# Two-layer streaming trunk on one core: low parts and products moved to VectorE, and the last two w_down groups exchanged in size

## The chip, the cores and the metric

The kernel runs on one core of a Trainium2 chip, in one launch. The metric is the device time of a whole execution in microseconds (us), from the first to the last instruction of the program and what lies around it. The core has four computing engines with instruction streams of their own: TensorE (PE in the profile, with PEld for its weight loads), VectorE (DVE), ScalarE (ACT) and GpSimd (POOL); SyncE (SP) and GpSimd issue the DMA transfers.

## What is computed

Two layers over 576 tokens (64 of a later chunk, 512 of a first chunk), width 1024, feed-forward width 2816:

```
for l in range(2):
    xn = rmsnorm(x, norm_mix[l])
    x = x + merge_branches(three attentions of xn @ w_in[l]) 
    xn = rmsnorm(x, norm_ffn[l])
    gu = xn @ w_up[l]                        # (576, 2 * 2816)
    g, u = gu[:, :2816], gu[:, 2816:]
    c = conv_b + causal 3-tap convolution of g along the tokens
    x = x + (gelu(c) * u) @ w_down[l]
y = rmsnorm(x, norm_final)
```

The change lies in the feed-forward part of each layer, from `xn @ w_up` to the sum with `w_down`.

## The kernel before

Data lie transposed: 128 features on the partitions, 576 tokens along the row; `x` is eight such tiles, the feed-forward width 22 (f = 0 to 21). A float32 product is made from two rounded parts each: a high part (hi, a rounded copy) and a low part (lo, what the rounding left), and three matmuls of 128x128 by 128x288: hi by hi, hi by lo, lo by hi. `scalar.copy` makes a high part, a subtraction on VectorE the low one.

The first NORD = 4 tiles of each layer are made in the old form (`ffn_f`): 48 matmuls for the gate half (mg), 48 for the up half (mu), then the convolution (c, two VectorE passes of 128x578), gelu (ge on ScalarE), the product with `ur`, and the parts `hh` and `hl`. Meanwhile `forms` prepares block sums of x for the other 18 tiles (fh and fl). These are made as block products (`unit_f`): seven products of half size, A11, P, R, A12, Q, A22, V in this order, with 12 matmuls each, 84 for a tile. Their weights are sums of quarter blocks of w_up: `wforms` loads them (wr), adds them on VectorE and spawns `wparts`, which makes the parts: piece a holds A11 and A12 (whi..a, wlo..a), b holds P and R (eh..b, el..b), c holds Q and V (whi..c, wlo..c), d holds A22 (eh..d, el..d). The high and low tiles of a have two buffers that a and c share, so whi of tile f waits for A12 of tile f - 1. A low part is made in one of two ways:

```
def low(out, src, hi, by_dma):
    if by_dma:
        scalar.activation(out, hi.bitcast(F32), AF.Copy, scale=-1.0)
        charge("POOL", 900)
        nc.gpsimd.dma_start(out, src, accum_op=ALU.add)
    else:
        vector.tensor_tensor(out, src, hi.bitcast(F32), op=ALU.subtract)
```

The last product of a tile, V, gives the second half of the gate (gp); then follow c on ScalarE (one pass) and VectorE (two), gelu, ge * u, hh and hl.

The down product `x += hh, hl by w_down` (md, weights dr and dh, dl, or wrd and whid, wlod) runs in groups of f tiles, in four pieces d2 of two x tiles each: 12 matmuls for an x tile and group tile, so a piece has 24 matmuls in a group of two and 48 in a group of four. Between block-product tiles stands one piece of an earlier group. The last group ends the layer: in layer 0 each finished x tile gets its parts for the next layer's products (xhm on ScalarE, xlm on VectorE, squares added on GpSimd into accm), and the next products are mv1a; in layer 1 `down_final` goes through the last group by halves of the tokens and each finished half tile goes into facc and xg, then come transposes (y), the sum over the partitions (frp), the scale rr and the outputs.

The order of instructions on each engine is fixed when the program is built: steps are written as generators, and a planner with a clock per engine and costs per operation (`charge`) decides which generator goes next. On the chip every engine takes its instructions strictly in that order.

Of the kernel before, what the change touches and what calls it, by code (L numbers as in the profile page):

```python
# [14 lines left out]
ALU = mybir.AluOpType  # L15
# [23 lines left out]
EARLY = 2  # L39
XACT = ()  # L40
XADD = 3
FG = [2, 2, 4, 4, 4, 4, 2]
NORD = 4
GW = TOK + 4

# [2 lines left out]
def trunk_kernel(ctx: ExitStack, tc: tile.TileContext, a: dict, o: dict):  # L48
# [91 lines left out]
    vector = Engine(nc.vector, "DVE", dve_cost)  # L140
    gpsimd = Engine(nc.gpsimd, "POOL", pool_cost)
# [10 lines left out]
    def spawn(label, g, first=False):  # L152
        gens.insert(0 if first else len(gens), [label, g, cx["t"]])
# [1038 lines left out]
    def layer(l):  # L1192
# [65 lines left out]
        def ffn_f(f):  # L1258
            nm = f"{l}f{f}"
            t = {}  # L1260

            def pre():
                drain(f"f{l}{f - 2}")
                gp = slot(f"gp{nm}", w=GW)
                t["gp"] = gp
                gpsimd.tensor_copy(gp[:, 0:2], state(l, f))
                gpsimd.memset(gp[:, 66:68], 0.0)

            def evg(j, ps, cs, h):
                gp, R = t["gp"], cur["R"]  # L1270
                if h == 0:
                    vector.tensor_tensor(gp[:, 2:66], ps[:, 0:T], R[:, 0:T], op=ALU.mult)
                    vector.tensor_tensor(gp[:, 68:292], ps[:, T:HALF], R[:, T:HALF], op=ALU.mult)
                else:
                    vector.tensor_tensor(gp[:, 292:580], ps, R[:, cs], op=ALU.mult)

            def conv():
                t["ge"] = yield from conv_steps(f, t["gp"])

            def pre_u():  # L1280
                t["ur"] = ap_.tile([P, TOK], F32, tag="g", name=f"ur{nm}", bufs=2)

            def evu(j, ps, cs, h):
                vector.tensor_tensor(t["ur"][:, cs], ps, cur["R"][:, cs], op=ALU.mult)

            def fin():
                ge = t["ge"][:, 0:TOK]
                gpsimd.tensor_tensor(ge, ge, t["ur"], op=ALU.mult)
                yield
                h_, l_ = slot(f"hh{nm}", F32R), slot(f"hl{nm}", F32R)  # L1290
                scalar.copy(h_, ge)
                yield
                vector.tensor_tensor(l_, ge, h_.bitcast(F32), op=ALU.subtract)
                hs[f] = (h_, l_)

            chunk(f"g{nm}", a["w_up"][l][:, f * P:(f + 1) * P], ND, act, evg, pre_ev=pre,
                  pre=begin_ffn if f == 0 else (lambda: spawn("wf", wforms())) if f == NORD - 1 else None, norm=[1] if f == 0 else None,
                  post=lambda: (spawn(f"c{l}{f}", conv()), spawn("forms", forms()) if f == 0 else None))

            def post_u():  # L1300
                drain(f"c{l}{f}")
                spawn(f"f{l}{f}", fin())

            chunk(f"u{nm}", a["w_up"][l][:, F + f * P:F + (f + 1) * P], ND, act, evu, pre_ev=pre_u, post=post_u,
                  pre=(lambda: fast.update(last=True)) if f == NORD - 1 else None)
# [65 lines left out]
        def wparts(f, nm, forms_, src, by_dma, small):  # L1371

            if f > NORD:
                yield from until(lambda: all((f - 1, n) in used for n in forms_))
            elif nm == "a":
                yield from until(lambda: "last" in fast)
            elif nm in "cd":
                yield from until(lambda: "go" in fast)
            yield
            key = f"{l}{f}{nm}"  # L1380
            if small:
                pairs = [(half_tile(f"eh{key}{j}", F32R), half_tile(f"el{key}{j}", F32R))
                         for j in range(len(forms_))]
            else:
                h_, l_ = (wp.tile([P, 8, P], F32R, tag=t, name=f"{t}{key}", bufs=2) for t in ("whi", "wlo"))
                pairs = [(h_[:, 4 * j:4 * j + 4, :], l_[:, 4 * j:4 * j + 4, :]) for j in range(2)]
            for j, n in enumerate(forms_):
                hi, lo = pairs[j]
                scalar.copy(hi, src[:, 4 * j:4 * j + 4, :])
                yield  # L1390
                low(lo, src[:, 4 * j:4 * j + 4, :], hi, by_dma)
                ws[f, n] = (hi, lo)
                made.add((f, n))
                yield

        def wforms():

            w = a["w_up"][l]
            rr = lambda t: t.rearrange("(k p) c -> p k c", p=P)
            for f in range(NORD, NF):  # L1400
                gc, uc = w[:, f * P:(f + 1) * P], w[:, F + f * P:F + (f + 1) * P]

                def raw(i, *need):
                    if f > NORD:
                        yield from until(lambda: all((f - 1, n) in made for n in need))
                    return wp.tile([P, 8, P], F32, tag="raw", name=f"wr{l}{f}{i}", bufs=3)

                r1 = yield from raw(1, "P", "R")
                dma(r1[:, 4:8, :], rr(uc[0:D // 2]))
                r0 = yield from raw(0, "A11", "A12")  # L1410
                dma(r0, rr(gc))
                if f > NORD:
                    yield from until(lambda: (f - 1, "A22") in made)
                a22 = half_tile(f"wr{l}{f}3")
                dma(a22, rr(uc[D // 2:D]))
                yield from pause(6000)
                vector.tensor_tensor(r1[:, 0:4, :], r1[:, 4:8, :], a22, op=ALU.add)
                yield
                vector.tensor_tensor(r1[:, 4:8, :], r1[:, 4:8, :], r0[:, 0:4, :], op=ALU.add)
                yield  # L1420
                spawn("wa", wparts(f, "a", ("A11", "A12"), r0, f != NORD + 1, False), True)
                spawn("wb", wparts(f, "b", ("P", "R"), r1, False, True), True)
                spawn("wd", wparts(f, "d", ("A22",), a22, True, True), True)
                q = yield from raw(2, "Q", "V")
                vector.tensor_tensor(q[:, 0:4, :], r1[:, 0:4, :], r0[:, 0:4, :], op=ALU.add)
                yield
                vector.tensor_tensor(q[:, 4:8, :], q[:, 0:4, :], r0[:, 4:8, :], op=ALU.add)
                yield
                spawn("wc", wparts(f, "c", ("Q", "V"), q, False, False), True)
# [132 lines left out]
        def down(fs, last):  # L1562
            def ev(d2):
                def go(j, ps, cs, h):
                    d = 2 * d2 + j
                    if fs[0] == 0:
                        drain_while(lambda: fast.get("y", -1) < d % 4, "y")
                        cx["t"] = clk["PE"] + 70
                    vector.tensor_tensor(x[d][:, cs], ps, x[d][:, cs], op=ALU.add)
                    if last and h == 1:  # L1570
                        norm_tile(f"m{l + 1}", d, x[d], gmix(l + 1, d))
                        dma(xsp[d], x[d])
                return go

            if last or fs[0] == 0:
                for d2 in range(4):
                    chunk(f"d{l}{fs[0]}{d2}", down_w(fs, d2), len(fs),
                          lambda: ([hs[f][0] for f in fs], [hs[f][1] for f in fs]), ev(d2), ncol=2,
                          pre=down_pre(fs, d2, last))
                return  # L1580
            for d2 in range(4):
                yield
                own = fs is not groups[-2] or d2 < 2
                chunk(f"d{l}{fs[0]}{d2}", down_w(fs, d2), len(fs),
                      lambda: ([hs[f][0] for f in fs], [hs[f][1] for f in fs]), ev(d2), ncol=2,
                      pre=down_pre(fs, d2, last), post=lambda n=len(owns): issued.add(n), own=own)
                if own:
                    owns.append((chunks[-1], fs, d2))
# [18 lines left out]
        groups = []  # L1607
# [7 lines left out]
            for n, (c, fs, d2) in enumerate(owns):  # L1615
                yield from down_own(c, fs, d2, lambda: n == 0 or n - 1 in issued)

        downs = iter(())
        for gi, fs in enumerate(groups):
            for i, f in enumerate(fs):  # L1620
                if f < NORD:
                    ffn_f(f)
                    if gi and i == 0:
                        list(downs)
                    continue
                chunk(f"x{l}{f}", None, 0, lambda f=f: (f == NORD and start_fast(), unit_f(f)), None, own=True)
                next(downs, None)
            list(downs)
            downs = down(fs, False)
            if gi:  # L1630
                next(downs)

        def start_fast():
            drain("forms")
# [368 lines left out]
```

## Time and profile before

| | |
|---|---|
| median of 3 runs | 2208.74 us (2205.34 to 2210.13) |
| profiled execution | 2207.59 us |
| its span, first to last instruction | 2205.7 us |
| TensorE busy | 2111.8 us (96%) |
| VectorE, ScalarE, GpSimd busy | 1514.3, 1228.5, 425.3 us |
| granted TensorE clock, mean | 0.984 of full |

The rows below come from the profiled execution; 1.9 us of its time lie outside its span. A busy share near the whole says which engine sets the time, and what is to be had lies where that engine waits.

### The profile page before, as it was taken

How to read it: one execution, taken by the hardware profiler on the slowest of the kernel's cores; microseconds unless marked ns; L12 is line 12 of the kernel's file. 1: busy time of each engine (PE TensorE's matmuls, PEld its weight loads, DVE VectorE, ACT ScalarE, POOL GpSimd, SP SyncE). 2: the span in 40 equal slices, each digit the busy share in tenths (PEclk: the TensorE clock that was granted, in tenths of full speed). 3: DMA queues.
4: the chain of work that ended last, by engine and by line, in shares of the span. 5: the costliest groups of instructions: out<-in, count | busy, mean ns of one | idle time of the engine just before them, and what ended most of it. 6: DMA issues, size and time to landing. Idle time of an engine off the chain costs nothing.

```text
span 2205.7 us, 40108 instructions
## 1 busy us (share of the span) xinstructions
PE 2111.8 (96%) x15479; PEld 2069.2 (94%) x15479; DVE 1514.3 (69%) x3148; ACT 1228.5 (56%) x2485; POOL 425.3 (19%) x615
## 2 busy tenths in 40 slices
PE   8999999999999879999899999999999998799997
PEld 7999999999999779999899999999999997699997
DVE  7886657676558657777568766677765686567775
ACT  5657766555436435555346677755554464455554
POOL 2111221111213212222101122202102231221121
PEclk9999999999999989999999999999999999899999
DMA  7442222232424436556243322233323264456551
GB/s 216 124 144 70 79 81 78 83 104 83 129 78 114 114 92 148 134 137 142 80 117 95 97 71 71 71 102 90 96 77 120 86 131 102 101 142 146 129 125 59
DMA packets 346280, 234.87 MB, mean 106 GB/s; under 512 B 13872, under 2 KB 324082, under 8 KB 346026
## 3 DMA queue, kind: packets, MB, share of 16 engines
q1 hardware_dynamic: 325898, 194.88, 30.1%
q0 software_dynamic: 20192, 37.43, 9.5%
q8 instruction: 122, 2.00, 0.4%
q14 instruction: 68, 0.56, 0.1%
HBM read 176.54 MB, written 25.83 MB: 92 GB/s over the span
## 4 chain that ended last, share of the span: by engine, by line
PE 83%; DVE 5%; issue 5%; DMA 4%; ACT 2%; POOL 1%; SPq 0%; POOLq 0%; DVEq 0%; ACTq 0%
PE md L146 10%; PE mo L146 4%; PE mg1a L146 2%; PE mg0a L146 2%; PE mg1b L146 2%; PE mg0b L146 2%; PE mg1c L146 2%; PE mg0c L146 2%; PE mv1a L146 1%; PE mb0a L146 1%; PE mb1a L146 1%; PE mv1b L146 1%; PE mv0b L146 1%; PE mv0c L146 1%; PE mv1c L146 1%
## 5 line engine op out<-in xcount | busy, mean ns | idle before, releaser
L117 DVE TENSOR_TENSOR wr<-wr,wr 128x512 f32<-128x512 f32 x144 | 98.7, 688 | 69.2 <-DMA wr<-in_w_up 68.0
L117 DVE TENSOR_TENSOR x<-md,x 128x288 f32<-128x288 f32 x224 | 98.4, 453 | 37.2 <-PE md L146 36.8
L146 PE MATMUL mo<-ml,whio 128*128 128x288 f32 x256 | 75.8, 296 | 0.8 <-DVE ml L117 0.8
L146 PE MATMUL md<-hh0f,dl 128*128 128x288 f32 x256 | 75.6, 295 | 0.5 <-DVE dl L117 0.5
L146 PE MATMUL md<-hh1f,dl 128*128 128x288 f32 x256 | 75.6, 295 | 0.5 <-DVE dl L117 0.5
L146 PE MATMUL mo<-mh,whio 128*128 128x288 f32 x256 | 75.8, 296 | 0.0
L146 PE MATMUL md<-hh0f,dh 128*128 128x288 f32 x256 | 75.5, 295 | 0.0
L146 PE MATMUL md<-hl1f,dh 128*128 128x288 f32 x256 | 75.5, 295 | 0.0
L146 PE MATMUL md<-hh1f,dh 128*128 128x288 f32 x256 | 75.5, 295 | 0.0
L146 PE MATMUL md<-hl0f,dh 128*128 128x288 f32 x256 | 75.5, 295 | 0.0
L146 PE MATMUL mo<-mh,wloo 128*128 128x288 f32 x256 | 75.4, 295 | 0.0
L117 DVE TENSOR_TENSOR dl<-dr,dh 128x512 fp32r<-128x512 f32 (+1 forms) x72 | 45.2, 628 | 19.8 <-ACT dh L117 19.8
L146 PEld LDWEIGHTS mo<-ml,whio 128*128 128x128 f32 x256 | 48.2, 188 | 1.2 <-DVE ml L117 1.2
L146 PEld LDWEIGHTS md<-hh1f,dl 128*128 128x128 f32 x256 | 48.2, 188 | 0.8 <-DVE dl L117 0.8
L146 PEld LDWEIGHTS md<-hh0f,dl 128*128 128x128 f32 x256 | 48.2, 188 | 0.8 <-DVE dl L117 0.8
L146 PEld LDWEIGHTS md<-hh1f,dh 128*128 128x128 f32 x256 | 48.2, 188 | 0.0
L146 PEld LDWEIGHTS mo<-mh,wloo 128*128 128x128 f32 x256 | 48.2, 188 | 0.0
L146 PEld LDWEIGHTS md<-hl0f,dh 128*128 128x128 f32 x256 | 48.2, 188 | 0.0
L146 PEld LDWEIGHTS md<-hh0f,dh 128*128 128x128 f32 x256 | 48.1, 188 | 0.0
L146 PEld LDWEIGHTS md<-hl1f,dh 128*128 128x128 f32 x256 | 48.1, 188 | 0.0
L146 PEld LDWEIGHTS mo<-mh,whio 128*128 128x128 f32 x256 | 48.1, 188 | 0.0
L117 ACT ACTIVATE xhf<-x,pcol 128x576 fp32r<-128x576 f32 x16 | 12.5, 780 | 63.9 <-DVE x L117 63.9
(2902 smaller groups left out, 9493.1 us busy)
## 6 DMA issues: line engine op xcount, KB each, us to landing
wr<-in_w_up SPq DMA_DIRECT2D x72, 256.0 KB
wr<-in_w_up SPq DMA_DIRECT2D x36, 512.0 KB
dr<-in_w_down SPq DMA_DIRECT2D x56, 256.0 KB
wro<-in_w_out SPq DMA_DIRECT2D x16, 512.0 KB
xspill<-x SPq DMA_DIRECT2D x16, 288.0 KB
x<-xspill SPq DMA_DIRECT2D x16, 288.0 KB
wrg0a<-in_w_in SPq DMA_DIRECT2D x8, 512.0 KB
wrg0b<-in_w_in SPq DMA_DIRECT2D x8, 512.0 KB
```

Source lines behind the costliest of these rows:

```text
L117: return f(*args, **kw)
L146: nc.tensor.matmul(out, lhsT=lhsT, rhs=rhs, start=start, stop=stop, skip_group_check=True)
```

## The change

Three edits. The product `ge * ur` of the four old-form tiles of each layer goes from GpSimd to VectorE. The low parts of piece a go to VectorE for f = 4 to 9; before, VectorE made them for f = 5 alone and an accumulating DMA from GpSimd's queue for the others. The last two groups of w_down become two and four tiles, where they were four and two; the loop that puts pieces between tiles keeps a list of groups with open pieces, so that after tile 16 and 17 there stand pieces 0 and 1 of group 12 to 15, after 18 and 19 pieces 2 and 3 of it, after 20 and 21 pieces 0 and 1 of group 16 and 17, then its pieces 2 and 3, then the group of 18 to 21.

```diff
-FG = [2, 2, 4, 4, 4, 4, 2]
+FG = [2, 2, 4, 4, 4, 2, 4]
...
-                gpsimd.tensor_tensor(ge, ge, t["ur"], op=ALU.mult)
+                vector.tensor_tensor(ge, ge, t["ur"], op=ALU.mult)
...
-                spawn("wa", wparts(f, "a", ("A11", "A12"), r0, f != NORD + 1, False), True)
+                spawn("wa", wparts(f, "a", ("A11", "A12"), r0, f > NORD + 5, False), True)
...
-        downs = iter(())
+        waiting = []
         for gi, fs in enumerate(groups):
             for i, f in enumerate(fs):
                 if f < NORD:
                     ffn_f(f)
-                    if gi and i == 0:
-                        list(downs)
+                    if gi == 1 and i == 0:
+                        list(down(groups[0], False))
                     continue
                 chunk(f"x{l}{f}", None, 0, lambda f=f: (f == NORD and start_fast(), unit_f(f)), None, own=True)
-                next(downs, None)
-            list(downs)
-            downs = down(fs, False)
-            if gi:
-                next(downs)
+                if waiting and next(waiting[0], "end") == "end":
+                    waiting.pop(0)
+            if 0 < gi < len(groups) - 1:
+                waiting.append(down(fs, False))
+                next(waiting[-1])
+        for g in waiting:
+            list(g)
```

On VectorE, between V of tile 5 and the middle of tile 6 in layer 0, there stood before (gp is the second gate half of tile 5, x<-md the four evictions of the down piece, wr the sums for tile 6):

```order
L117 TENSOR_TENSOR gp0f_9073<-m0f5V,z0f_8882 128x288
L117 TENSOR_TENSOR wr_9218<-wr_9110,wr_9112 128x512
L117 TENSOR_TENSOR x_02_7486<-md_9214,x_02_7486 128x288
L117 SCALAR_TENSOR_TENSOR c0f_9220<-gp0f_9073,pcol_1178,c0f_9220 128x578 x2
L117 TENSOR_TENSOR x_02_7486<-md_9230,x_02_7486 128x288
L117 TENSOR_TENSOR el06b_9238<-wr_9110,eh06b_9237 128x512
L117 TENSOR_TENSOR wr_9218<-wr_9218,wr_9112 128x512
L117 TENSOR_TENSOR x_03_7488<-md_9253,x_03_7488 128x288
L117 TENSOR_TENSOR x_03_7488<-md_9263,x_03_7488 128x288
```

and in the change:

```order
L117 TENSOR_TENSOR gp0f_9071<-m0f5V,z0f_8876 128x288
L117 TENSOR_TENSOR wr_9216<-wr_9108,wr_9110 128x512
L117 TENSOR_TENSOR x_02_7486<-md_9212,x_02_7486 128x288
L117 SCALAR_TENSOR_TENSOR c0f_9218<-gp0f_9071,pcol_1178,c0f_9218 128x578 x2
L117 TENSOR_TENSOR x_02_7486<-md_9228,x_02_7486 128x288
L117 TENSOR_TENSOR el06b_9236<-wr_9108,eh06b_9235 128x512
L117 TENSOR_TENSOR wr_9216<-wr_9216,wr_9110 128x512
L117 TENSOR_TENSOR x_03_7488<-md_9251,x_03_7488 128x288
L117 TENSOR_TENSOR wlo06a<-wr_9110,whi06a 128x512
L117 TENSOR_TENSOR x_03_7488<-md_9260,x_03_7488 128x288
```

The low part wlo06a has come in behind the third eviction; nothing else has moved there. One tile later, on VectorE from the convolution of tile 6 to the first parts of tile 7, there stood before:

```order
L117 SCALAR_TENSOR_TENSOR c0f_9419<-gp0f_9271,pcol_1178,c0f_9419 128x578 x2
L117 TENSOR_TENSOR x_04_7490<-md_9429,x_04_7490 128x288
L117 TENSOR_TENSOR el07b_9437<-wr_9307,eh07b_9436 128x512
L117 TENSOR_TENSOR wr_9417<-wr_9417,wr_9320 128x512
L117 TENSOR_TENSOR x_05_7492<-md_9452,x_05_7492 128x288
L117 TENSOR_TENSOR x_05_7492<-md_9462,x_05_7492 128x288
L117 TENSOR_TENSOR dl_9484<-dr_9355,dh_9482 128x256
L117 TENSOR_TENSOR ge0f_9487<-ge0f_9487,u0f_9275 128x576
L117 TENSOR_TENSOR el07b_9439<-wr_9307,eh07b_9438 128x512
```

and in the change:

```order
L117 SCALAR_TENSOR_TENSOR c0f_9412<-gp0f_9268,pcol_1178,c0f_9412 128x578 x2
L117 TENSOR_TENSOR wr_9302<-wr_9302,wr_9332 128x512
L117 TENSOR_TENSOR x_04_7490<-md_9422,x_04_7490 128x288
L117 TENSOR_TENSOR x_05_7492<-md_9431,x_05_7492 128x288
L117 TENSOR_TENSOR x_05_7492<-md_9439,x_05_7492 128x288
L117 TENSOR_TENSOR wr_9460<-wr_9302,wr_9332 128x512
L117 TENSOR_TENSOR ge0f_9447<-ge0f_9447,u0f_9272 128x576
L117 TENSOR_TENSOR dl_9457<-dr_9363,dh_9455 128x256
L117 TENSOR_TENSOR el07b_9466<-wr_9302,eh07b_9465 128x512
L117 TENSOR_TENSOR wr_9460<-wr_9460,wr_9332 128x512
L117 TENSOR_TENSOR wlo07a<-wr_9332,whi07a 128x512
```

Two sums wr that stood ahead of gp have moved behind the convolution, ge stands ahead of the first el07b, and wlo07a comes last; tile 8 is ordered as tile 6. On ScalarE at tile 10 (c and ge are those of tile 9), the change has:

```order
L117 ACTIVATE c0f_10030<-gp0f_9891,pcol_1028,pcol_1178 128x578
L117 CAST eh010d_10042<-wr_9937 128x512
L117 CAST eh010b_10045<-wr_9913 128x512
L117 CAST whi010a<-wr_9935 128x512
L117 ACTIVATE el010d_10043<-eh010d_10042 128x512
L117 ACTIVATE wlo010a<-whi010a 128x512
```

This is the order that tile 9 had before; before the change whi010a and the first step of wlo010a stood ahead of c at tile 10.

## Rows read from the trace of the kernel before

**Rows 1.** Page, busy time and its share; costliest groups, busy us and mean ns.

```profile
PE 2111.8 (96%) x15479; PEld 2069.2 (94%) x15479; DVE 1514.3 (69%) x3148; ACT 1228.5 (56%) x2485; POOL 425.3 (19%) x615
...
L117 DVE TENSOR_TENSOR wr<-wr,wr 128x512 f32<-128x512 f32 x144 | 98.7, 688 | 69.2 <-DMA wr<-in_w_up 68.0
```

**Rows 2.** Waits of TensorE, whole span: us in total, times, longest.

```profile
PE md L146 <- DVE wlod L117: 9.3, 2, 5.8
...
PE md L146 <- DVE x L117: 4.0, 3, 1.8
...
PE m0f9A L146 <- DMA wlo09a<-wr: 2.6, 1, 2.6
...
PE m0f5A L146 <- DVE wlo05a L117: 2.2, 1, 2.2
...
PE m0f4A L146 <- DMA wlo04a<-wr: 1.4, 2, 0.7
```

**Rows 3.** Stretches: length, busy us (count) by engine, granted clock, DMA share, GB/s.

```profile
726.20:857.55 131.35, 105.09 (x698) 101.58 (x697) 79.73 (x143) 58.35 (x124) 26.02 (x46) 0.91 0.47 109
743.60:762.10 18.50, 16.33 (x108) 15.89 (x108) 14.52 (x28) 8.11 (x19) 1.86 (x5) 0.91 0.32 86
762.10:786.75 24.65, 17.80 (x109) 17.08 (x108) 12.59 (x24) 9.21 (x21) 3.65 (x7) 0.86 0.38 86
837.20:857.55 20.35, 17.80 (x134) 17.56 (x133) 13.87 (x27) 11.14 (x23) 6.61 (x10) 1.00 0.74 157
857.55:875.00 17.45, 17.45 (x134) 17.45 (x133) 13.00 (x25) 10.13 (x20) 3.54 (x7) 1.00 0.59 142
1815.95:1948.40 132.45, 106.00 (x699) 102.44 (x698) 80.40 (x143) 58.22 (x124) 25.98 (x46) 0.91 0.47 109
1061.15:1120.20 59.05, 46.66 (x295) 45.41 (x294) 34.40 (x64) 22.13 (x39) 9.17 (x7) 0.86 0.29 91
2152.20:2205.70 53.50, 40.92 (x301) 38.27 (x300) 29.72 (x62) 24.96 (x57) 10.37 (x13) 0.95 0.19 60
```

**Rows 4.** Timeline at tiles 6, 7, 9 of layer 0: start, us, instruction, idle before.

```profile
767.98 0.61 PE L146 MATMUL m0f6A<-fh,wlo06a 128*128 128x288 f32 x1 [5.32 <-DMA wlo06a<-wr]
792.62 0.61 PE L146 MATMUL m0f7A<-fh,wlo07a 128*128 128x288 f32 x1 [5.33 <-DMA wlo07a<-wr]
840.20 0.40 PE L146 MATMUL m0f9A<-fh,wlo09a 128*128 128x288 f32 x1 [2.55 <-DMA wlo09a<-wr]
763.71 0.82 DVE L117 TENSOR_TENSOR x<-md,x 128x288 f32<-128x288 f32 x2
790.07 0.69 DVE L117 TENSOR_TENSOR el07b<-wr,eh07b 128x512 fp32r<-128x512 f32 x1
836.86 0.45 DVE L117 TENSOR_TENSOR x<-md,x 128x288 f32<-128x288 f32 x1
```

**Rows 5.** Timeline of VectorE and GpSimd at an old-form product.

```profile
673.60 0.45 DVE L117 SCALAR_TENSOR_TENSOR tp<-tp,yb 128x288 f32<-128x288 f32 x1
674.08 1.57 DVE L117 TENSOR_TENSOR tq<-tp,yb 128x288 f32<-128x288 f32 x1
673.83 1.50 POOL L117 TENSOR_TENSOR ge0f<-ge0f,ur0f 128x576 f32<-128x576 f32 x1 [4.12 <-DVE ur0f L117]
```

**Rows 6.** Timeline of VectorE at the end of layer 0.

```profile
1088.41 0.82 DVE L117 SCALAR_TENSOR_TENSOR xlm<-x,pcol,xhm 128x576 fp32r<-128x576 f32 x1 [0.85 <-ACT xhm L117]
...
1090.81 0.82 DVE L117 SCALAR_TENSOR_TENSOR xlm<-x,pcol,xhm 128x576 fp32r<-128x576 f32 x1 [0.84 <-ACT xhm L117]
1091.54 1.62 DVE L117 TENSOR_TENSOR wlod<-wrd,whid 128x256 fp32r<-128x256 f32 x1
```

**Rows 7.** Timeline, the last eviction of x, and the chain that ended last behind it.

```profile
2191.39 0.46 DVE L117 TENSOR_TENSOR x<-md,x 128x288 f32<-128x288 f32 x1 [0.35 <-PE md L146]
...
2194.77 2.98 PE y L150 x25
2197.76 0.51 PE frp L146 x6
```

## The prediction

> **What bounds the kernel now.** I read the page's busy times first: TensorE is busy for 2111.8 us of 2205.7, VectorE for 1514.3 [rows 1]. So there are some 94 us in which TensorE stands still, and beside them only what it loses at a lower clock. The list of TensorE's waits says for what it stands: low parts of piece a that come by accumulating DMA (wlo04a, wlo09a and others of their kind), wlo05a from VectorE, and md waiting for wlod and for x [rows 2]. The third view, busy time by stretch, shows where. Tile 10 of layer 0 has no gap: 84 matmuls of the tile and 48 of a down piece in 17.45 us, 0.132 us for one, at granted clock 1.00 [rows 3]. A tile with a piece of 24 is then 108 × 0.1322 = 14.28 us of work, and tiles 4 to 9 (four with 24, two with 48) are 4 × 14.28 + 2 × 17.45 = 92.0. They took 131.35 us in layer 0 and 132.45 in layer 1, at granted clock 0.91: losses of 39.3 and 40.4 [rows 3]. The end of layer 0, from V of tile 21 to the middle of mv1a, took 59.05 us for 295 matmuls (39.0 of work), the end of layer 1 53.5 us [rows 3]. These four stretches hold most of what is lost, and the change touches each.
>
> **What a tile's loss is made of.** Tile 6 took 24.65 us, 10.4 over its work: a wait of 5.32 for wlo06a, and 4.4 to 5 that no wait covers, at granted clock 0.86 (1.2 GHz for part of the tile, 2.4 for the rest) [rows 3, 4]. Tile 9 waited 2.55 and lost 20.35 − 17.45 = 2.9 in all, at granted clock 1.00; tile 5 waited 2.2 for a low part that VectorE makes already, and lost 18.5 − 14.28 = 4.2 [rows 2 to 4]. A wait of some 2 us thus brings 0.35 to 2.0 more, mean 1.2; one of 5 brings over 4.
>
> **Low parts of piece a.** Tile 5 had its low part on VectorE before, so five tiles of a layer change. Each loses two scaled copies on ScalarE and two accumulating DMAs from GpSimd's queue, and gains two subtractions on VectorE. I price one as the sum wr of the same shape, two inputs in SBUF, 688 ns [rows 1]: 20 more, 14 us in 2200 on an engine 69% busy. What counts is where they stand in its order.
> - Tile 6: PE would take the low at 767.98 − 5.32 = 762.66. The low now stands behind the third eviction; the double row of the last two starts at 763.71, so the third ends near 764.15, the low near 764.8 [rows 4]. Wait 2.1, with 1.2 behind it 3.3 (before 10.4).
> - Tile 7: PE is ready at 792.62 − 5.33 = 787.29. Before, the last el07b ended at 790.07 + 0.69 = 790.76 [rows 4]. Now two wr have come behind the convolution (+1.38), a first-parts el fewer stands ahead (−0.69) and the low comes last (+0.69): 790.8 if the queue's own idle time takes the wr up, 792.1 if not: a wait of 3.5 to 4.8. I take 4.7, since gp and the convolution ahead leave the queue no slack, and 2.0 behind it: 6.7.
> - Tile 8 has tile 6's order: 3.3.
> - Tile 9: ready at 840.20 − 2.55 = 837.65; the eviction ends at 836.86 + 0.45 = 837.31, two wr and the low follow, 839.2 [rows 4]. Wait 1.5 and 0.4: 1.9.
> - Tile 4: two waits of 0.7 before [rows 2]; I leave 1.0 (bounds 0 to 3). Tile 5: nothing of its own changes, 4.2.
> - Tile 10 is still by DMA, but ScalarE now starts its first step where it started tile 9's, behind c and two casts. So the wait of tile 9, 2.55, and 0.35 to 2.0 more, goes there: 3.7, where nothing was lost before [rows 3, 4].
>
> After: 1.0 + 4.2 + 3.3 + 6.7 + 3.3 + 1.9 + 3.7 = 24.1. Layer 0 gains 39.3 − 24.1 = 15, layer 1, with the same orders, 40.4 − 24.1 = 16: together **31**. With every low like tile 7's the loss is 3 × 3 ≈ 10 larger for a layer; with waits of nothing behind the third eviction it is 6 smaller.
>
> **Old-form products.** A 128x288 operation on VectorE with two inputs in SBUF took 0.45 us alone, and 1.57 while GpSimd's product of 1.50 us ran [rows 5]. So a product of twice as many columns costs VectorE 0.7 to 0.9 and gives back about 1.1. Nothing in the first four tiles of TensorE waits for it but md of group 0, which waited up to 1.8 for x once in each layer [rows 2]. I take a gain of 1 per layer, **2** (bounds: −1, if the products only stand in VectorE's way, to 3.6, if both waits go).
>
> **End of layer 0.** Before, a finished x tile came every 12 matmuls, 1.6 us, but VectorE and ScalarE pass each tile to one another (xhm on ScalarE, 0.85 idle, then xlm, 0.82), and two xlm start 1088.41 and 1090.81, 2.4 us apart [rows 6]. TensorE then starves, 59.05 − 39.0 = 20 us in all, 9.3 of it in two waits of md for wlod, whose subtraction stands in the same queue of VectorE [rows 2, 3]. With four tiles in the last group an x tile takes 24 matmuls, 3.2 us, above 2.4 + 0.7 for one of the two low parts of 512 columns that each piece now needs. The tiles' number of matmuls stays the same. What ends later is the tail of tile 21 (c, gelu, ge, hh, hl): it has 48 matmuls of pieces 2 and 3 and 24 to 36 of tiles 18 to 20 ahead of it, about 9.5 us, and TensorE waits for none of it unless that tail takes longer. I take that the ping-pong's loss goes and 4 us remain: **16** (bounds: 0, below under the first rival, to 18).
>
> **End of layer 1.** Its window held 53.5 us [rows 3]: 39.2 to the last md (240 md, 31.7, and 30 transposes, 3.6, so 3.9 lost) and 14.3 from there, of which 2205.7 − 2198.27 = 7.4 lie behind frp [rows 7]. After: 24 more md stand in the window, since a piece of two fewer stood ahead of V (3.2 us, which the stretch ahead gives back), so 53.5 + 3.2 = 56.7 is to be compared. 264 × 0.1322 = 34.9, the early transposes 3.6 (0.119 each, by y x25 in 2.98 [rows 7]), frp 0.5, waits 1.3 (a third of before): 40.3. Behind the last md come 15 transposes, 1.8, an eviction, 0.5, and the 7.4 again: 9.9 with rounding. 56.7 − 50.2 = **6** (bounds 0 to 9).
>
> **Sum.** 31 + 2 + 16 + 6 = 55 from 2207.59 (span 2205.7 and 1.9 outside it; the median of the runs is 2208.74): **2153**.
>
> **A rule against it.** The row of tile 6 shows 4.4 to 5 us lost beyond its wait, at granted clock 0.86, that of tile 9 0.35 at 1.00 [rows 3, 4]; I priced the coming waits like the shorter ones. The Trainium skill, in "TensorE: Matmul & The Clock Gate", section "HAM oscillation — how this bites in real kernels", says that a wait in every round makes each round start at the lower clock again, so that the transition is paid every time. This case's trace agrees at tile 6 and not at tile 9. By the rule the change would still leave waits in tiles 6 to 10, each with tile 6's price behind it. That is the third rival below, worked out from tile 6's row.
>
> **The rivals.**
> 1. *The layer ends give back little.* Place: VectorE and ScalarE behind the last group. An xlm has ScalarE's 0.85 ahead of it and takes 0.82; with two evictions of 0.45 and a 512-wide low of 0.69 that is 3.26, about the 3.2 that TensorE now needs. But a 256-wide wlod among GpSimd's adds took 1.62 [rows 6], where half of 0.69 and overhead would be 0.4: stretched by 1.2. A 512-wide one stretched so makes 4.45 a tile, and 8 × (4.45 − 3.2) = 10 of the 16 are gone; the same wait in layer 1 takes 5 of its 6. 2153 + 15 = 2168. For it: the 1.62, and that the whole chain goes through one engine. Against it: only some lows fall beside an add.
> 2. *Every low waits like tile 7's.* VectorE takes its orders in sequence, and the evictions ahead wait for TensorE themselves; 10 a layer minus what tile 9 keeps, 6 to 7: 2153 + 13 = 2166. For it: 69% busy on average is more in these tiles; against it: the rows of tile 6 leave only 2.1.
> 3. *Each wait costs the lower clock.* Behind the waits of 6, 7, 8, 9 and 10 stand 4.4 us instead of 1.2, 2.0, 1.2, 0.4, 1.2: 16 a layer, 32 in both: 2185. For it: tile 6 at 0.86; against it: tile 9 at 1.00 after 2.55, and tile 5 at 0.91.
> 4. *Slower than before.* If the clock does not come back to 2.4 GHz between these waits, because now one lies in every tile from 4 to 10 and none runs through, a tile of 14.28 takes as much again. From 55/14.28 = 3.9 such tiles on the change loses; all twelve from 4 to 9 would cost 171 and give 2324. Before, tiles 6 to 8 had longer waits and still got 0.86 in a row, which speaks strongly against it.
>
> That the change does little where it says most is part of this: tile 5 was on VectorE already, and tile 10 takes over the wait that tile 9 loses.
>
> **How the numbers follow.** Forecast 0.60 (its own range 2138 to 2162), rival 1 0.15, rival 2 0.10, rival 3 0.06, larger gain than the bounds of 16 and 31 let me take 0.04 (2130), rival 4 or an end that loses 0.05. The range 2136 to 2178 holds the first three and part of the larger gain, some 0.87 by these cases, which I let stand as 8 in 10 since their prices are bounds from few rows. A measurement of this kernel can tell about 0.2%, 4.4 us, from no change: faster 0.93, within it 0.02, slower 0.05.
>
> **What would show it.** Right: tiles 6 and 8 of both layers at 17 to 18 us, tile 7 near 21, tile 10 near 21 with a DMA wait of 2 to 3 on wlo010a; xlm at the end of layer 0 at even steps of some 3.2 us with TensorE waiting for little between them, and the window at 43; 10 us from the last md to the end. Wrong: waits of 4 or more for VectorE's wlo06a and wlo08a (rival 2), granted clock under 0.9 at tiles with waits of 2 (rival 3), xlm or wlod of over 1.5 us and md waiting for x or wlod in the last group (rival 1). A wait that the order does not show, such as hl of tile 21 coming behind the lows of the last group, would break the term of 16 first.

## The result and the profile after

The change took 2158.49 us (median of 4, 2157.9 to 2160.29) against 2207.04 for the kernel before (4 runs): a ratio of 0.9775, 95% interval 0.9764 to 0.9787, 48.5 us less. Forecast were 2153 and a gain of 55, within a range of 2136 to 2178. In the later rounds the kernel before had medians of 2209.4 to 2209.9; beside those the gain would be 51. The span of the profiled execution fell from 2205.7 to 2156.1.

The page's busy times after (before: [rows 1]):

```profile
PE 2097.5 (97%) x15479; PEld 2057.5 (95%) x15479; DVE 1513.8 (70%) x3176; ACT 1216.1 (56%) x2465; POOL 386.0 (18%) x587
```

VectorE has 28 instructions more and the same busy time. With one edit at a time (the runs below) it was 1524.6 us with the lows, 1506.3 with the product and 1510.4 with the groups, against 1514.3 before: the lows cost it 10.3, and the other two give that back. Busy times say little here; the stretches do (before: [rows 3]). First tiles 4 to 9 of layer 0, then its tiles 5 to 10 one by one, tiles 4 to 9, 5 and 10 of layer 1, and the ends of layer 0 and layer 1 (length, busy us and count of PE, PEld, DVE, ACT, POOL, granted clock, DMA share, GB/s):

```profile
725.56:839.47 113.91, 99.29 (x699) 96.13 (x697) 83.28 (x152) 52.66 (x115) 13.89 (x33) 0.96 0.39 97
741.54:758.64 17.10, 14.82 (x109) 14.35 (x108) 14.64 (x28) 8.22 (x20) 1.84 (x5) 1.00 0.36 93
758.64:775.85 17.21, 15.01 (x109) 14.43 (x108) 12.53 (x25) 6.57 (x15) 2.00 (x7) 1.00 0.36 92
775.85:796.93 21.08, 16.76 (x109) 16.18 (x108) 13.40 (x27) 8.42 (x19) 1.61 (x3) 0.84 0.33 88
796.93:820.25 23.32, 19.73 (x135) 19.38 (x134) 17.22 (x31) 11.51 (x25) 1.84 (x5) 0.93 0.30 80
820.25:839.47 19.22, 17.83 (x134) 17.59 (x133) 15.28 (x28) 10.37 (x23) 3.92 (x7) 1.00 0.42 107
839.47:861.30 21.83, 19.32 (x134) 19.09 (x134) 14.48 (x26) 10.99 (x23) 5.53 (x10) 0.92 0.69 150
1783.38:1900.57 117.19, 101.27 (x699) 98.81 (x697) 83.05 (x151) 52.09 (x114) 12.87 (x33) 0.94 0.37 95
1801.80:1820.27 18.47, 16.31 (x109) 15.84 (x108) 14.47 (x28) 8.04 (x19) 1.84 (x5) 0.91 0.33 87
1900.57:1922.42 21.85, 19.31 (x135) 19.07 (x134) 14.56 (x26) 11.01 (x24) 5.54 (x10) 0.92 0.71 152
1044.08:1088.39 44.31, 43.61 (x319) 42.42 (x318) 34.29 (x64) 23.31 (x39) 8.89 (x7) 1.00 0.45 141
2105.27:2156.10 50.83, 43.09 (x327) 41.47 (x325) 27.82 (x62) 26.75 (x57) 10.90 (x13) 0.97 0.25 80
```

Tiles 4 to 9 fell from 131.35 to 113.9 us in layer 0 and from 132.45 to 117.2 in layer 1, and each layer gave 4.4 back at tile 10 (21.8 instead of 17.45). The end of layer 0 fell from 59.05 to 44.3 with 24 matmuls (3.2 us) more in it, so by 18; that of layer 1 from 53.5 to 50.8, likewise with 3.2 more, so by 6. TensorE's longest waits in the block-product tiles, where before the lows by DMA stood at 5.3 [rows 4]:

```profile
PE m1f7A L146 <- ACT whi17a L117: 2.7, 1, 2.7
PE m0f7A L146 <- ACT whi07a L117: 2.7, 1, 2.7
PE m1f10A L146 <- DMA wlo110a<-wr: 2.5, 1, 2.5
PE m0f10A L146 <- DMA wlo010a<-wr: 2.5, 1, 2.5
...
PE m1f4A L146 <- DMA el14d<-wr: 2.3, 1, 2.3
...
PE m0f8A L146 <- DVE wlo08a L117: 2.2, 1, 2.2
...
PE m0f6A L146 <- DVE wlo06a L117: 2.2, 1, 2.2
...
PE m0f7A L146 <- DVE wlo07a L117: 1.6, 1, 1.6
PE m0f8A L146 <- ACT whi08a L117: 1.4, 1, 1.4
...
PE m0f9A L146 <- DVE wlo09a L117: 1.4, 1, 1.4
```

No md waits for wlod at the end of layer 0 any more. The wait for whi07a, a cast on ScalarE, has grown from 0.8 us to 2.7, and one for whi08a has come in; for tiles 7 and 8 the prediction had looked at VectorE alone.

### The profile page after: what moved, and what is told of

It is laid out like the page before. It is cut to its first block, busy times and chain, and to the rows that moved or that the text cites. A ratio compares the mean times of both kernels' runs of the same rounds, so it can differ in the third digit from the quotient of the medians.

```text
span 2156.1 us, 40054 instructions
## 1 busy us (share of the span) xinstructions
PE 2097.5 (97%) x15479; PEld 2057.5 (95%) x15479; DVE 1513.8 (70%) x3176; ACT 1216.1 (56%) x2465; POOL 386.0 (18%) x587
## 4 chain that ended last, share of the span: by engine, by line
PE 85%; DVE 8%; DMA 2%; issue 2%; ACT 2%; POOL 1%; SPq 0%; DVEq 0%; ACTq 0%; POOLq 0%
PE md L146 8%; PE mo L146 4%; PE mg1b L146 2%; PE mg1a L146 2%; PE mg0a L146 2%; PE mg0b L146 2%; PE mg1c L146 2%; PE mg0c L146 2%; DVE x L117 1%; PE mb1a L146 1%; PE mb0a L146 1%; PE mv1b L146 1%; DMA wr<-in_w_up 1%; PE mv0b L146 1%; PE mv1c L146 1%
## 5 line engine op out<-in xcount | busy, mean ns | idle before, releaser
L146 PE MATMUL md<-hh0f,dl 128*128 128x288 f32 x240 | 70.8, 295 | 0.6 <-DVE dl L117 0.6
L146 PE MATMUL md<-hl0f,dh 128*128 128x288 f32 x240 | 70.9, 295 | 0.0
L146 PE MATMUL md<-hh0f,dh 128*128 128x288 f32 x240 | 70.8, 295 | 0.0
L146 PE MATMUL md<-hh1f,dl 128*128 128x288 f32 x240 | 70.8, 295 | 0.0
L146 PE MATMUL md<-hl1f,dh 128*128 128x288 f32 x240 | 70.8, 295 | 0.0
L146 PE MATMUL md<-hh1f,dh 128*128 128x288 f32 x240 | 70.8, 295 | 0.0
L117 DVE TENSOR_TENSOR dl<-dr,dh 128x512 fp32r<-128x512 f32 (+1 forms) x72 | 42.9, 596 | 10.9 <-ACT dh L117 10.9
```

Source lines behind the costliest of these rows:

```text
L117: return f(*args, **kw)
L146: nc.tensor.matmul(out, lhsT=lhsT, rhs=rhs, start=start, stop=stop, skip_group_check=True)
```

## The experiments

**Do the three edits add?** Each alone, on the kernel before. In all that follows a ratio is to the kernel before of the same round, with its 95% interval.

```diff
a1_lows:    -r0, f != NORD + 1, False    +r0, f > NORD + 5, False
a2_groups:  -FG = [2, 2, 4, 4, 4, 4, 2]  +FG = [2, 2, 4, 4, 4, 2, 4]  and the new loop
a3_product: -gpsimd.tensor_tensor(ge, ge, t["ur"]  +vector.tensor_tensor(ge, ge, t["ur"]
```

a1_lows: 

> The kernel before with the second edit alone: piece a's low parts on VectorE for tiles 4 to 9. Theory (the terms stand apart and add): tiles 4 to 10 gave back 13.0 us in layer 0 and 10.9 in layer 1 between the two traces, so 24 us: about 2183, with the layer ends as before (59 and 53.5 us). Rival (the groups' new places help the tiles too, by other pieces between them): under 18 us, above 2189. If the lows also empty the queues towards the ends, over 28, below 2179.

a2_groups: 

> The change without the lows and without the product: groups 2, 2, 4, 4, 4, 2, 4 and the new loop alone. Theory: the two layer ends alone, 18.0 and 6.0 us between the two traces, so 24 us: about 2183, tiles 4 to 10 as before (148.8 and 149.9 us for tiles 4 to 10). Rival (the end of layer 0 was helped by what the freed GpSimd and ScalarE no longer do): under 18, above 2189.

a3_product: 

> The kernel before with the first edit alone: the product of the old-form tiles on VectorE. Theory: md of group 0 waits 0.9 instead of 1.8 in each layer and nothing else changes: 2 us, about 2205, inside 0.2% of before. Rival (products stand in VectorE's way ahead of the first low parts): 0 to 2 us slower. More than 4 us either way would be a cost or gain that neither names.

Beside a before of 2209.57: lows 2185.22 (ratio 0.9893, 0.9878 to 0.9908), groups 2185.42 (0.9890, 0.9874 to 0.9905), product 2209.35 (0.9998, 0.9989 to 1.0007). That is 24.4 + 24.1 + 0.2 = 48.7 us, against 48.5 for the whole change beside its own before and 51 beside this one: they add, within intervals of some 3 us. The product is worth nothing that can be told; its interval, a loss of 1.5 us to a gain of 2.4, does not shut out the forecast 2. In its trace md of group 0 waits 0.88 instead of 1.75 in layer 0, and tiles 4 to 10 then take 149.7 where they took 148.8. That the time goes into the next stall, the lows by DMA, is not shown: with nothing changed in these tiles they took 148.6 in b1_nodep and 150.6 in b6_noadd.

**Does tile 10's wait pass on?** The change, with tile 10 on VectorE too (`f > NORD + 6`).

> The change with tile 10 on VectorE as well (tiles 4 to 10). Theory (tile 10 waits because its low comes by DMA behind the late cast, and tile 11 has its casts ahead of the convolution on ScalarE): the wait of 2.5 becomes tile 9's 1.4, the 1.8 behind it 0.4, and tile 11 waits for nothing: 2.5 us a layer, 5 in all, about 2153.5. Rival (the wait passes to the first tile that is left to the DMA): tile 11 waits about 2.5 for its low by DMA and the time stays within 2 us of 2158.5.

a4_low10 took 2148.70 (0.9728, 0.9715 to 0.9742), 9.8 us under the change. Tile 10 fell from 21.8 to 17.5 in both layers, with no wait at all, and tile 11 waits for nothing. The theory held in kind and its size was too small: I had left tile 10 the 1.4 that tile 9 waits. The rival falls.

**Why are tiles 7 and 8 late?** ScalarE and then VectorE at tile 7 after the change:

```profile
773.27 0.87 ACT L117 ACTIVATE c0f<-gp0f,pcol,pcol 128x578 f32<-128x578 f32 x1 [4.87 <-DVE gp0f L117]
775.89 0.78 ACT L117 ACTIVATE ge0f<-c0f 128x64 f32<-128x64 f32 x2 [1.74 <-DVE c0f L117]
...
777.90 0.61 ACT L117 CAST whi07a<-wr 128x512 fp32r<-128x512 f32 x1
...
774.18 1.68 DVE L117 SCALAR_TENSOR_TENSOR c0f<-gp0f,pcol,c0f 128x578 f32<-128x578 f32 x2
```

TensorE was ready for whi07a at 775.85. ScalarE had been idle for 4.87 us before the convolution and for 1.74 before gelu, each time waiting for VectorE, with the cast queued behind. The chain that ended last shows what this does to tile 8:

```profile
783.82 0.40 ACT s0f L117
784.22 0.53 ACT eh07b L117
...
784.77 0.70 DVE el07b L117
...
785.49 0.38 SPq L1409
...
787.50 6.45 DMA wr<-in_w_up
...
793.97 0.70 DVE wr L117
```

The second el07b is late, so the wr buffer that it reads comes free late, the load for tile 8 is issued at 785.5 only, its sums stand ahead of gp in VectorE's queue, and convolution and whi08a follow. b2_gelu puts gelu of tile 6 behind the casts of tile 7:

```diff
+            if late:    # late = (f == NORD + 2)
+                yield from until(lambda: (f + 1, "A11") in made)
             ge = slot(f"ge{nm}")
```

> The change, with gelu of tile 6 put behind the casts of tile 7 on ScalarE. Theory (whi07a comes 2.7 us late because gelu, waiting for VectorE's convolution, stands ahead of the casts; and tile 8 is late because the second eh07b stands behind the copy of tile 7's first product, so that SyncE starts tile 8's load late): tile 7 becomes like tile 6, 17.2 to 18.6 us instead of 21.1, and tile 8 loses its wait of 1.0 to 1.4 for whi08a; some 5 us a layer, 10 in all, about 2148. Rival (gelu's own tail, hh and hl of tile 6, is then what is late, or tile 8's casts): under 3 us in all, 2155 or more.

b2_gelu took 2150.50 (0.9738, 0.9725 to 0.9752): 8 of the 10 us. Tile 8 fell from 23.3 to 21.6 and from 22.9 to 20.4, without a wait for whi08a. Tile 7 only reached 19.7, since VectorE's wlo07a then was late by 3.2: it still stands behind the convolution and the evictions. The two tiles are best taken together, since a longer tile 7 leaves tile 8 less to wait for (20.8 us and then 2.2 for whi08a in layer 0 of a4_low10, 22.3 and 0.2 for whi18a in layer 1): without this edit they took 44 to 46 us in every trace with the change's lows on VectorE (a1_lows, a4_low10, b5_d4, c3_after_nodep and the change), with it 41.2 and 39.9.

**What would no low at all give, and what is the next wait?**

```diff
b3_nolow: -low(lo, ...)  +if nm == "a" and f <= NORD + 6: lo = hi
b5_d4:    -wparts(f, "d", ("A22",), a22, True, True)  +wparts(f, "d", ("A22",), a22, f > NORD, True)
```

> The change without the low parts of piece a in tiles 4 to 10: the high tile is used in the low one's place, so neither VectorE nor a DMA makes them (that part of the computation is left out). Theory (what is still lost in these tiles is the wait for the lows and the clock behind it; the casts are late only at tiles 7 and 8): the losses of 26 and 30 us fall to 3 to 8 a layer, 40 to 50 us, 2110 to 2120. Rival (the casts are as late as the lows were, since convolution, gelu and casts share ScalarE): 25 us at most, 2133 or more.

b3_nolow took 2107.64 (0.9539, 0.9526 to 0.9552), 51 us under the change and so a little more than the theory's 50: tiles 4 to 7 took 14.6 to 15.2, the granted clock over tiles 4 to 10 was 1.00, and no wait for a cast over 0.3 was left. Tiles 4 to 10 of layer 0:

```profile
725.44:837.65 112.21, 111.71 (x831) 110.03 (x830) 89.99 (x165) 62.42 (x133) 15.89 (x41) 1.00 0.51 128
```

With the lows gone the casts come in another order too, so this bounds what all of piece a costs, not the lows alone.

b5_d4: 

> The change, with piece d's low part of tile 4 (el..d) on VectorE too. Theory (with wlo14a on time, el14d by DMA is the next that is late at tile 4 of layer 1, 2.3 us, with 1.5 to 2 behind it): tile 4 of layer 1 falls from 18.4 to about 15, 3 us in all, about 2155. Rival (the wait passes on to tile 5, whose wlo15a is behind more on VectorE): within 2 us of 2158.5.

b5_d4 took 2155.48 (0.9759, 0.9746 to 0.9772). Tile 4 of layer 1 fell from 18.4 to 15.0, without a wait for el14d, and tile 5 of layer 1 stayed at 18.6, so the wait did not pass on to it as the rival has it. The size is less sure: with el14d left to the DMA that tile 4 took 16.2 in a4_low10 and 16.7 in c3_after_nodep. The interval overlaps that of the change, so the 3 us in all stay unproven.

**Engine or place?** c1_early10 is the change with tile 10 on VectorE and piece a started ahead of the sums wr; c4_earlydma is the kernel before, lows by DMA, groups and products untouched, with that one line moved.

```diff
                 yield from pause(6000)
+                spawn("wa", wparts(f, "a", ("A11", "A12"), r0, ..., False), True)
                 vector.tensor_tensor(r1[:, 0:4, :], r1[:, 4:8, :], a22, op=ALU.add)
...
-                spawn("wa", wparts(f, "a", ("A11", "A12"), r0, ..., False), True)
```

c1_early10: 

> The change with lows of tiles 4 to 10 on VectorE and with piece a's cast and low started before the sums wr instead of behind them. On ScalarE the first whi then stands ahead of the convolution and on VectorE its low right behind gp, in every tile alike. Theory (what counts for the waits is the place of the cast in the two queues): no tile waits for a low, little for el..b (0.3 to 0.5), tiles of 84 and 24 at 14.7 to 15.5 us: 40 to 48 us under the change, 2110 to 2120, near the 2107.6 without these lows. Rival (cast and low ahead of the convolution make c, gelu and the parts of the next tile late instead): 20 us at most, 2138 or more.

c4_earlydma: 

> The kernel before, lows still by DMA except tile 5, groups and products as before; only piece a's cast and low are started before the sums wr. Theory (place, not engine): cast and first step stand ahead of the convolution on ScalarE, the DMA of 3.3 us lands before the down piece is through, and 50 to 70 of the 80 us lost in tiles 4 to 9 come back: 2140 to 2158. Rival (engine: the way by DMA is too long wherever it starts): at most the 24 us that VectorE brought, 2185 or more.

c1_early10 took 2120.66 (0.9596, 0.9583 to 0.9609), 38 us under the change and the fastest kernel here that computes everything. c4_earlydma took 2150.24 (0.9729, 0.9716 to 0.9743): 59.6 us by one moved line, where the lows on VectorE had brought 24. With the lows of tiles 4 to 10 on VectorE the same line is worth 28 (a4_low10 to c1_early10). ScalarE at tile 6 in c4_earlydma, and VectorE there in c1_early10:

```profile
755.75 0.62 ACT L117 CAST whi06a<-wr 128x512 fp32r<-128x512 f32 x1 [1.46 <-DMA wr<-in_w_up]
756.40 0.63 ACT L117 ACTIVATE wlo06a<-whi06a 128x512 fp32r<-128x512 f32 x1
758.94 0.87 ACT L117 ACTIVATE c0f<-gp0f,pcol,pcol 128x578 f32<-128x578 f32 x1 [1.90 <-DVE gp0f L117]
```

```profile
755.01 0.45 DVE L117 TENSOR_TENSOR gp0f<-m0f5V,z0f 128x288 f32<-128x288 f32 x1
755.38 0.68 DVE L117 TENSOR_TENSOR wlo06a<-wr,whi06a 128x512 fp32r<-128x512 f32 x1
```

Cast and first step now fill the time in which ScalarE waits for gp. Tiles 4 to 10 of layer 0, c4_earlydma first, then c1_early10:

```profile
726.53:847.17 120.64, 114.04 (x831) 111.58 (x830) 92.93 (x166) 69.17 (x145) 28.22 (x53) 0.99 0.60 139
725.72:843.26 117.54, 111.97 (x830) 110.07 (x830) 97.38 (x178) 62.92 (x134) 16.69 (x41) 1.00 0.47 119
```

Tiles 5 to 10 of both layers took 203.4 us in c4_earlydma and 203.7 in c1_early10: there it makes no difference that can be told which engine makes the low. The whole 5 us between the two in tiles 4 to 10 lie in tile 4, where c4_earlydma still waits 1.4 for wlo04a and 0.7 for wlo14a by DMA, and in layer 0 1.8 for dl from VectorE; no run takes these apart. The theory of c4_earlydma held, in kind and in size (50 to 70 forecast). That of c1_early10 held in kind, none of tiles 4 to 10 waits for a low of piece a, and came out a little short: 38 instead of 40 to 48, since the second el..b waits 1.0 to 1.3 in tiles 5 to 8 where 0.3 to 0.5 was forecast. Both rivals fall.

**What starved TensorE at the end of layer 0?** b1_nodep takes ScalarE's xhm out of xlm on the kernel before, c3_after_nodep does so on the change, b6_noadd is b1_nodep without GpSimd's adds.

```diff
-in1=h.bitcast(F32), op0=ALU.mult   +in1=x if nm == "m1" else h.bitcast(F32), op0=ALU.mult
b6_noadd: +if nm != "m1" or d == ND - 1:   (ahead of the add into acc)
```

b1_nodep: 

> The kernel before, in which xlm of layer 1's first products is worked out from x alone and no longer from xhm, so that VectorE doesn't wait for ScalarE there (the low part is wrong with that; same instructions, same order). Theory (the passing to and fro of xhm and xlm, 2.4 us for an x tile against 1.6 of matmuls, is what starves TensorE at the end of layer 0): without the 0.85 the period is about 1.6, and 12 or more of the 20 us come back: about 2195. Rival (TensorE waits because wlod stands behind a burst of evictions, whoever made it late): 5 us at most, 2203 or more.

b6_noadd: 

> b1_nodep with GpSimd's six adds of squares left out at the end of layer 0 as well (the sum of squares is replaced by a scaled first square, so the norm is wrong too; VectorE's order is that of before). b1_nodep took 7.9 us off the window from V to mk1a, of about 20 lost. Theory A (the rest is the place of wlod and wlov1a in VectorE's queue, behind the evictions and xlm of the piece ahead): the waits of 3.1, 1.5 and 3.5 stay within 1.5 us each, 1 to 3 us in all, about 2198. Theory B (the rest is GpSimd's adds, beside which xlm took 1.9 instead of 0.8): 6 us or more, 2194 or less.

c3_after_nodep: 

> The change, with xlm of layer 1's first products from x alone as in b1_nodep (the low part is wrong with that). Before the change this took 9.3 us off. Theory (24 matmuls an x tile, 3.2 us, cover the to and fro of xhm and xlm): nothing left to gain, within 1.5 us of 2158.5. Rival (the end of layer 0 is still paced by VectorE): 3 to 6 us faster.

b1_nodep took 2200.38 (0.9958, 0.9945 to 0.9972), b6_noadd 2200.24 (0.9948, 0.9935 to 0.9962), c3_after_nodep 2156.43 (0.9756, 0.9743 to 0.9770). The window from V of tile 21 to mk1a, the product behind mv1a, before, in b1_nodep and in b6_noadd:

```profile
1059.56:1120.27 60.71, 48.32 (x308) 47.07 (x307) 35.05 (x66) 22.13 (x39) 9.17 (x7) 0.86 0.28 89
1059.06:1111.89 52.83, 44.76 (x308) 43.81 (x306) 35.08 (x66) 22.01 (x39) 9.28 (x7) 0.94 0.33 102
1063.28:1114.02 50.74, 44.46 (x308) 43.44 (x307) 32.56 (x66) 21.99 (x39) 0.59 (x1) 0.93 0.34 108
```

It fell from 60.7 to 52.8 and to 50.7. So the to and fro is 8 of the 20 us, between the two expectations of b1_nodep: neither its theory nor its rival was the whole. TensorE's waits in that window, b1_nodep first, then b6_noadd:

```profile
PE md L146 <- DVE wlod L117: 4.6, 2, 3.1
PE mv1a L146 <- DVE wlov1a L117: 3.5, 1, 3.5
```

```profile
PE md L146 <- DVE wlod L117: 3.2, 2, 1.7
PE mv1a L146 <- DVE wlov1a L117: 3.1, 1, 3.1
```

GpSimd's adds cost 2 us of this window (the two medians, 0.1 apart, don't show it), and 10 us stay with both gone: 6.3 of waits and the rest at a granted clock of 0.93. The waits moved by less than 1.5 us each, as theory A says. That they come from the place of wlod and wlov1a in VectorE's queue, behind the evictions and xlm of the piece ahead, is read from the order; no run moved them. On the change c3_after_nodep has no such wait left to lose; its window is 44.5 against 45.9, so 1.4 shorter. Its median is 2.1 under the change, a little outside the theory's 1.5, but the intervals overlap: the cover of 24 matmuls does what was said, as far as these runs can tell.

## Why the prediction was right, and where it was off

- **End of layer 0, 16; measured 18.** Right in size, but the mechanism was only half named, so the closeness is in part luck. The step put the whole 16 down to the to and fro of xhm and xlm; the runs showed that as 8 of 20, GpSimd's adds as 2, and 10 in waits for wlod and wlov1a and the lower clock behind them. Twice the matmuls for an x tile covers all of these, and a2_groups shows it by itself, with the same window as the change, 45.9. xlm did not come at even steps of 3.2 either, but in pairs 2.4 us apart with 6.9 from pair to pair: the to and fro is still there and is covered. "The tiles' number of matmuls stays the same" was wrong for the window: 319 stand in it, not 295.
- **End of layer 1, 6; measured 6.** Right in mechanism too: 9.9 us from the last md to the end, as forecast (14.3 before), and 40.9 up to it, where 40.3 was forecast.
- **Products, 2; measured 0.2,** with an interval that does not shut out 2. The wait did halve; booking it as time is what no run bears out.
- **Low parts, 31; measured 24 (13.0 and 10.9).** This is the mis-sized term. Losses over the tile's own work, in us:

| tile | forecast | layer 0 | layer 1 |
|---|---|---|---|
| 4 | 1.0 | 1.7 | 4.1 |
| 5 | 4.2 | 2.8 | 4.2 |
| 6 | 3.3 | 2.9 | 2.9 |
| 7 | 6.7 | 6.8 | 6.8 |
| 8 | 3.3 | 5.9 | 5.5 |
| 9 | 1.9 | 1.8 | 1.7 |
| 10 | 3.7 | 4.4 | 4.4 |

The step that failed is "Tile 8 has tile 6's order: 3.3": that holds on VectorE, and wlo08a waits 2.2 as wlo06a does, but ScalarE and SyncE set when tile 8 could start, and the cast whi08a adds a wait of 1.4. (The text also expected 17 to 18 us for tile 8, which with a piece of 48 was 20.8 by its own sum.) The other is tile 4 in layer 1, where el14d by DMA waited 2.3; the list of waits before had it already, with 1.2, and the sum left it out. Tile 7 came out to 0.1, by another division, 2.7 for a cast and 1.6 to 1.9 for the low instead of 4.7 for the low, and by luck: in the other traces with these orders it lost 6.5 to 8.0 and tile 8 lost 4.3 to 6.3.

The forecast also read one row too high. The stretch of 24.65 us for tile 6 reaches into a wait of tile 7, and tile 6 has a second wait. From the list of waits before:

```profile
PE m0f6A L146 <- DMA wlo06a<-wr: 6.0, 2, 5.3
...
PE m1f4A L146 <- DMA el14d<-wr: 1.2, 1, 1.2
...
PE m0f7A L146 <- ACT whi07a L117: 0.8, 1, 0.8
```

Without that 0.8 the tile took 23.8, and 3.5 of it, not 4.4 to 5, no wait covers. This makes rival 3 cheaper than its 2185; the sum does not use it.
- **Tile 10** took over a wait of 2.5 from the DMA, as read from ScalarE's order.
- **The rivals.** Rival 1 did not cost anything, though what it names was there: beside GpSimd's adds three of the six 512-wide lows between the xlm took 1.4 to 1.6 us instead of 0.7. No md waited for them; the one wait left in the end of layer 0 is 0.5 for xlm. Rival 2 is refuted (2.2 for wlo06a and wlo08a), rival 4 did not come. Rival 3 came in part: tiles 7, 8 and 10 ran at 0.84, 0.93 and 0.92 and lost 1.8 to 2.5 beyond their waits, tiles 5, 6 and 9 of layer 0 at 1.00 and lost some 0.4 to 0.7. The Trainium skill ("TensorE: Matmul & The Clock Gate", "HAM oscillation — how this bites in real kernels") tells of a kernel in which a wait in every round, longer than any single one left in these tiles, makes each round start at the lower clock. With the waits of 1.4 to 2.7 in this trace that came in some tiles and not in others.

## What to carry to other kernels

When TensorE waits for a part that another engine makes, look first at what stands ahead of that part in its engine's queue and for what that waits. Here the place of piece a's casts and lows was worth 60 us with the lows by DMA (28 with them on VectorE), the choice of engine 24, and with the right place the engine made no difference in tiles 5 to 10. When one stall is removed, read every queue on the way to the next tile (here ScalarE's and SyncE's), not only the one that was edited. Widen the work per output tile where another chain of engines sets its pace: that covers several causes at once.

## What the runs showed of the hardware

The same wait has several prices. Tile 5 waits 2.17 us for wlo05a (in layer 1 2.16 for wlo15a) in every run with the change's lows late in the queue, and took 17.10 us at granted clock 1.00 and 18.47 at 0.91 in the rows above, and in b5_d4:

```profile
740.94:760.84 19.90, 17.63 (x109) 17.16 (x108) 14.66 (x28) 8.24 (x20) 1.85 (x5) 0.83 0.30 80
```

So up to 2.8 us of a tile of 17 hang on whether TensorE is granted 1.2 GHz for a while after the gap instead of 2.4; what decides it no run here shows.

xlm took 0.82 alone and 1.90 beside GpSimd's add in b1_nodep, and 0.82 for each of eight in b6_noadd. The slow one and its add:

```profile
1085.48 1.90 DVE L117 SCALAR_TENSOR_TENSOR xlm<-x,pcol 128x576 fp32r<-128x576 f32 x1
1085.33 1.43 POOL L117 TENSOR_TENSOR accm<-accm,sqm 128x576 f32<-128x576 f32 x1 [23.37 <-ACT sqm L117]
```

The Trainium skill ("SBUF — State Buffer", "Who interferes with whom") states that a VectorE instruction with two SBUF inputs contends with a GpSimd instruction that reads SBUF; the two traces agree.
